# Expert weights in 2 MiB transfers of 16 KB rows, with six ring places instead of twelve

## The chip, the cores and the metric

The kernel runs on one core of one Trainium2 chip. The metric is the device time of one execution in microseconds, as the median of several runs. One further execution was taken by the hardware profiler; the rows below are its.

## What is computed

Two layers of a diffusion backbone over 256 latent tokens and 256 context tokens with 1024 channels. Each layer mixes tokens (Fourier, neighbourhood attention, short convolution) and then channels. The channel mixer of layer 0 is a dense SwiGLU, that of layer 1 is a router with eight experts, of which each latent token uses two:

```python
def moe(h, w_router, w_gate, w_up, w_down):
    logits = (h @ w_router).astype(jnp.float32)
    top_val, top_idx = lax.top_k(logits, TOP_K)
    ...
    out = jnp.zeros_like(h)
    for e in range(N_EXPERTS):
        out = out + gates[..., e:e + 1] * swiglu(h, w_gate[e], w_up[e], w_down[e])
    return out
```

One expert has a gate and an up matrix of 1024 x 3584 and a down matrix of 3584 x 1024, all float32: 42 MiB. All eight experts are read in every execution, 336 MiB. The change is in how these weights reach SBUF; what is computed from them stays.

## The kernel before

**Steps.** An expert's 3584 inner channels are worked in seven chunks of 512 (FE = 7), so there are 56 steps (expert, chunk). A step uses three blocks of weights of 2 MiB: gate, up and, one step later, down. Experts are of two kinds, ABABABAB. An A expert may hold 128 tokens; its weights are split into a high and a low part (`split`, line 181: ACT copies to `wh`, DVE subtracts to `wl`), and each product is three matmuls (`mm3`, line 188). A B expert holds 64 tokens; PE reads its float32 weights from the raw tile directly (lines 1263 and 1303). `expert_steps` (line 266) gives the order: four A steps first, then B and A steps in turn, then the last four B steps.

**A step** (`step`, line 1342, in the function `experts`) does `gate_up` for its own chunk and then `down` for the step before it. Inside `gate_up`, PE also transposes the previous step's product (`turn`, line 1271; PE transposes, L1275). That product is the DVE multiplication at line 1269. After the last A chunk of an expert with a successor pair, `gather` (line 1197, matmuls at L1210) picks the rows of the next two experts. PE, ACT and DVE run in the order in which the program is written (`manual_schedule`).

**Weights.** `expert_plan` (line 274) lists the loads in the order in which PE uses them: every block as two halves of 1 MiB, 128 rows of 8 KB. Half n goes to place n mod 15. The places are twelve tiles of their own (`ring`, RING = 12, line 951) and the three buffers of `net.wraw`, which served the earlier layers. The first twelve loads are issued by POOL (the `aside` argument), all others by SP, in the order of the plan (`Stream.load`, line 73). Up to fifteen halves are asked for ahead of the one being made ready; the DMA into a place waits until the half before it there has been read. For an A half that is when DVE has finished the second of its two splits, for a B half when PE has done its matmuls. SP's queue is in order, so a load that waits for its place holds up those behind it.

**Splitting ahead.** `Stream.make` (line 98) writes the splits of A weights into ACT's and DVE's order up to four units (quarter blocks of 1024 columns) ahead of PE, because there are four `wh`/`wl` pairs. So the first splits of an A block `down` stand in the order of ACT and DVE before the multiplication of that A step, while PE uses that block only after the next B step's gate and up products.

**An expert's result.** `scatter` (line 1311) writes an expert's output to a tile with the tag `y` in the pool `pre`. The same memory held the router's input before (`Route.start`, line 1033).

The functions that the change touches, and those that call them, follow.

Of the kernel before, what the change touches and what calls it, by code (L numbers as in the profile page):

```python
# [8 lines left out]
F32 = mybir.dt.float32  # L9
# [10 lines left out]
P = 128  # L20
# [9 lines left out]
NE = 8  # L30
FE = 7
# [5 lines left out]
CAPS = (128, 128, 128, 64, 64, 64, 64)  # L37

LEAD = 4
RING = 12  # L40
SCRATCH = 2048
HALVES = 5

# [16 lines left out]
class Stream:  # L60


    def __init__(self, net, plan, ahead, parts, aside=0, before=8):

        self.aside, self.before = aside, before
        self.net, self.plan, self.ahead, self.parts = net, plan, ahead, parts
        self.units = [(i, j) for i, (_, _, nu, _, _) in enumerate(plan) for j in range(nu)]
        self.loaded, self.raws, self.halves = 0, {}, 0
        self.at, self.made, self.count, self.ready = 0, 0, 0, {}
        self.alive, self.kept, self.used = [], {}, []  # L70
        self.hold = len(self.units)

    def load(self, upto):
        nc = self.net.nc
        while self.loaded < min(upto, len(self.plan)):
            _, src, _, n, pool = self.plan[self.loaded]
            if pool is None:
                if self.halves == HALVES:
                    return
                self.halves += 1  # L80
            eng = nc.gpsimd if self.loaded < self.aside else nc.sync
            src = src() if callable(src) else src
            if pool is None:
                t = self.net.halves()
                for j in range(2):
                    eng.dma_start(t[j], src[:, j * D:(j + 1) * D])
            else:
                t = pool.tile([P, 2048], F32, tag="raw", name="raw")
                eng.dma_start(t[:, :n], src)
            self.raws[self.loaded] = t  # L90
            self.loaded += 1
# [6 lines left out]
    def make(self):  # L98

        net = self.net  # L100
        while self.made < self.hold:
            i, j = self.units[self.made]
            _, _, nu, n, _ = self.plan[i]
            whole = nu == 1
            if not whole and len(self.alive) == len(self.parts) or self.made > self.at + self.before:
                return
            self.load(i + self.ahead)
            if i not in self.raws:
                return
            raw = self.raws[i]  # L110
            if whole:
                self.ready[self.made] = raw
            else:
                m = n // nu
                wh, wl = self.parts[self.count % len(self.parts)]
                h = wh.tile([P, 1024], F32R, tag="wh", name="wh")
                lo = wl.tile([P, 1024], F32R, tag="wl", name="wl")
                net.split(h[:, :m], lo[:, :m], raw[:, j * m:(j + 1) * m])
                self.ready[self.made] = (h, lo)
                self.alive.append(self.made)  # L120
                self.count += 1
            if j == nu - 1:
                del self.raws[i]
            self.made += 1
# [141 lines left out]
def expert_steps(kinds):  # L266

    a, b = ([(e, f) for e in range(NE) if kinds[e] == x for f in range(FE)] for x in "AB")
    if not b:
        return a  # L270
    return a[:LEAD] + [x for y in zip(b, a[LEAD:]) for x in y] + b[len(a) - LEAD:]


def expert_plan(a, pools, kinds, expert):

    plan, n = [], 0
    steps = expert_steps(kinds)
    for i in range(len(steps) + 1):
        srcs = []
        if i < len(steps):  # L280
            srcs += [(x, *steps[i], hf) for x in "gu" for hf in range(2)]
        if i > 0:
            srcs += [("d", *steps[i - 1], hf) for hf in range(2)]
        for x, e, f, hf in srcs:
            src = lambda x=x, e=e, f=f, hf=hf: a[f"moe_{x}"][expert(e), f, hf]
            plan.append(((x, e, f), src, 2 if kinds[e] == "A" else 1, 2048, pools[n % len(pools)]))
            n += 1
    return plan


def build(nc, tc, a, out):
    with ExitStack() as es:
        net = Net(nc, tc, es, a)
# [651 lines left out]
        with late(name="own", bufs=8, side="right") as own:  # L945
            with late(name="den1", bufs=1) as den, late(name="act1", bufs=3) as act, late(name="tog", bufs=8) as tog:
                x = mixing(act, den, tog, tog, own, 1, 6, route.shifts)
            first.close()
            more = lambda **kw: es.enter_context(late(**kw))

            ring = [more(name=f"ring{i}", bufs=1) for i in range(RING)]
            pre = more(name="pre", bufs=1)
            pools = ring + [net.wraw] * 3
            parts = [(net.wh, net.wl)] * 4
            stream = lambda aside, kinds, expert: Stream(net, expert_plan(a, pools, kinds, expert), len(pools), parts,
                                                         aside, 20)
            route.start(pre, scales(1, 1, g2, 1))
            mixed(1, x, route.chunk)

# [99 lines left out]
def experts(net, pre, mo, res, mods, route, rt, ident, ones, tri, iot, sel8):  # L1059
# [176 lines left out]
    def run(st, kinds, more, Sums):  # L1236
# [7 lines left out]
        def gate_up(e, f, between):  # L1244
            pg = [net.bank(), net.bank()]
            t = sg[e, f] = net.t2()
            whole = kinds[e] == "B"
            n = 256 if whole else 512
            for i, name in enumerate("gu"):
                for kk in range(4):  # L1250
                    if not whole:
                        h, lo = st.next(name, e, f)
                        for j in range(2):
                            k, c = 2 * kk + j, slice(j * 512, j * 512 + 512)
                            net.mm3(pg[i], xa[0][:, k], xa[1][:, k], h[:, c], lo[:, c], k == 0, k == KD - 1)
                    else:

                        if kk % 2 == 0:
                            w = st.next(name, e, f)
                        for k in (2 * kk, 2 * kk + 1):  # L1260
                            for j in range(2):
                                c = (k % 4) * 512 + j * 256
                                nc.tensor.matmul(pg[i][j * half:(j + 1) * half, :256], xb[e][:, k], w[:, c:c + 256],  # L1263
                                                 start=k == 0, stop=k == KD - 1)
                    if (i, kk) in between:
                        between[i, kk]()
                if i == 0:
                    net.act(t[:, :n], pg[0][:, :n], AF.Silu)
            nc.vector.tensor_mul(t[:, :n], t[:, :n], pg[1][:, :n])  # L1269
# [14 lines left out]
        def down(e, f, between={}):  # L1284
            x = parts.pop((e, f))
            if f == 0:
                py[e] = [net.bank(), net.bank()]
            for n in range(2):
                for i in range(2):
                    if kinds[e] == "A":  # L1290
                        h, lo = st.next("d", e, f)
                        for j in range(2):
                            k, c = 2 * i + j, slice(j * 512, j * 512 + 512)
                            kc = slice(k * P, k * P + P)
                            net.mm3(py[e][n], x[0][:, kc], x[1][:, kc], h[:, c], lo[:, c],
                                    f == 0 and k == 0, f == FE - 1 and k == 3)
                    else:
                        if i == 0:
                            w = st.next("d", e, f)

                        for j in range(2):
                            k, c = 2 * j + i, i * P + j * half
                            nc.tensor.matmul(py[e][n][j * half:(j + 1) * half], x[:, c:c + half],  # L1303
                                             w[:, k * 512:(k + 1) * 512],
                                             start=f == 0 and i == 0, stop=f == FE - 1 and i == 1)
                    if (n, i) in between:
                        between[n, i]()
                if f == FE - 1:
                    scatter(e, n)
# [31 lines left out]
        y = {}  # L1341
# [52 lines left out]
def layout(i):  # L1394
# [4 lines left out]
    a = {}  # L1399
# [39 lines left out]
    a["router"][:, :, :NE] = i["moe_router"][0].reshape(KD, P, NE).transpose(1, 0, 2)  # L1439
    for n, s in (("moe_g", "moe_w_gate"), ("moe_u", "moe_w_up")):  # L1440
        w = i[s][0].reshape(NE, 2, 4, P, FE, 512)
        a[n] = c(w.transpose(0, 4, 1, 3, 2, 5).reshape(NE, FE, 2, P, 2048))
    w = i["moe_w_down"][0].reshape(NE, FE, 4, P, 2, 512)
    a["moe_d"] = c(w.transpose(0, 1, 4, 3, 2, 5).reshape(NE, FE, 2, P, 2048))


    rows = S // GW
# [44 lines left out]
```

## Time and profile before

| | us |
|---|---|
| median of three runs | 1854.37 |
| the three runs | 1853.98, 1854.37, 1857.76 |
| the profiled execution | 1857.7 |
| its span, first to last instruction | 1855.9 |
| PE busy in the span | 1827.5 (98%) |
| DVE busy | 1183.7 (64%) |
| ACT busy | 824.5 (44%) |
| mean granted TensorE clock | 0.996 |

DMA moved 514.69 MB, 277 GB/s on average. The span is what the rows of the profile are measured in: their times count from its first instruction. A busy PE is not a PE at its peak, since the ends of matmuls are modelled. An idle engine costs time only where the chain of waits runs through it.

### The profile page before, as it was taken

The numbers are of one execution on the slowest core, as the hardware profiler recorded it, in microseconds if no ns is written. First come the engines' busy times: TensorE is split into PE (matmuls) and PEld (weight loads), VectorE is DVE, ScalarE is ACT, GpSimd is POOL, SyncE is SP. The second block draws the span as 40 slices with busy tenths as digits, with TensorE's granted clock in tenths as the row PEclk, the third lists the DMA queues.
The fourth block names the chain that finished last, engine by engine and source line by source line (L and its number), as shares of the span: only waits on it lengthen the run. The fifth ranks groups of instructions, "written<-read, shape, count | busy, mean of one in ns | idle before, by whom it ended". The sixth has DMA issues, their size and how long they took to land.

```text
span 1855.9 us, 26261 instructions
## 1 busy us (share of the span) xinstructions
PE 1827.5 (98%) x10254; PEld 1438.4 (78%) x10254; DVE 1183.7 (64%) x1725; ACT 824.5 (44%) x1179; POOL 23.4 (1%) x49
## 2 busy tenths in 40 slices
PE   7999999999999999999999999999999999999997
PEld 5787888888888888898999877677676767667664
DVE  5658677759767474668567866565665656566542
ACT  3546322334222223355446755454554545455431
POOL 0000000000000000001000000000000000000000
PEclk9999999999999999999999999999999999999998
DMA  9322344434547463344756899999999999999994
GB/s 368 114 91 91 133 162 159 177 141 159 204 145 261 161 238 114 123 148 144 279 184 267 339 383 421 416 421 421 420 420 421 421 421 421 421 421 421 421 421 201
DMA packets 74355, 514.69 MB, mean 277 GB/s; under 512 B 8432, under 2 KB 8560, under 8 KB 14448
## 3 DMA queue, kind: packets, MB, share of 16 engines
q1 hardware_dynamic: 69840, 491.84, 67.4%
q0 software_dynamic: 4240, 20.97, 3.2%
q8 instruction: 82, 1.34, 0.3%
q14 instruction: 49, 0.40, 0.1%
q10 hardware_dynamic: 144, 0.13, 0.0%
HBM read 509.76 MB, written 1.05 MB: 275 GB/s over the span
## 4 chain that ended last, share of the span: by engine, by line
PE 92%; DMA 5%; DVE 2%; ACT 1%; issue 0%; SPq 0%; ACTq 0%; DVEq 0%
PE ps L190 23%; PE ps L191 23%; PE ps L192 23%; PE ps L1263 10%; PE ps L1303 5%; DMA raw<-in_moe_d 2%; PE ps L1275 1%; DMA raw<-in_moe_u 1%; DMA raw<-in_moe_g 1%; PE ps L641 1%; PE ps L617 1%; PE ps L653 1%; PE ps L1210 1%; DMA res<-in_xT 1%; PE ps L1332 0%; PE ps L342 0%
## 5 line engine op out<-in xcount | busy, mean ns | idle before, releaser
L183 ACT CAST wh<-raw 128x1024 fp32r<-128x1024 f32 (+1 forms) x524 | 544.9, 1049 | 654.3 <-PE ps L191 367.2
L186 DVE TENSOR_TENSOR wl<-raw,wh 128x1024 fp32r<-128x1024 f32 (+1 forms) x524 | 630.9, 1218 | 240.1 <-ACT wh L183 206.8
L190 PE MATMUL ps<-hh,wh 128*128 128x512 f32 (+1 forms) x1024 | 361.3, 355 | 1.4 <-ACT hh L170 1.4
L191 PE MATMUL ps<-hl,wh 128*128 128x512 f32 (+1 forms) x1024 | 361.0, 353 | 0.9 <-DVE hl L433 0.6
L192 PE MATMUL ps<-hh,wl 128*128 128x512 f32 (+1 forms) x1024 | 360.6, 353 | 0.0
L190 PEld LDWEIGHTS ps<-hh,wh 128*128 128x128 f32 x1024 | 192.7, 189 | 30.1 <-issue 2.0
L191 PEld LDWEIGHTS ps<-hl,wh 128*128 128x128 f32 x1024 | 193.6, 189 | 27.5 <-DVE hl L433 1.5
L192 PEld LDWEIGHTS ps<-hh,wl 128*128 128x128 f32 x1024 | 193.5, 189 | 26.6
L1263 PE MATMUL ps<-raw,xb 128*64 128x256 f32 x1792 | 208.8, 384 | 0.0
L1263 PEld LDWEIGHTS ps<-raw,xb 128*64 128x64 f32 x1792 | 125.8, 138 | 77.1 <-issue 20.8
L363 DVE CUSTOM_DVE_ANT_0 junk<-raw,csb,early 128x1024 bf16<-128x1024 f32 x128 | 164.2, 1282 | 32.7 <-DMA raw<-in_w_at 30.3
L190 PE MATMUL ps<-wh,xh 128*128 128x512 f32 x448 | 177.3, 396 | 0.0
L192 PE MATMUL ps<-wh,xl 128*128 128x512 f32 x448 | 174.7, 390 | 0.0
L191 PE MATMUL ps<-wl,xh 128*128 128x512 f32 x448 | 174.7, 390 | 0.0
L1269 DVE TENSOR_TENSOR t<-t,ps 128x512 f32<-128x512 f32 (+1 forms) x56 | 30.8, 551 | 113.0 <-PE ps L1263 113.0
L1303 PE MATMUL ps<-raw,t 128*64 128x512 f32 x448 | 102.2, 598 | 0.0
L192 PEld LDWEIGHTS ps<-wh,xl 128*128 128x128 f32 x448 | 84.1, 188 | 17.7
L191 PEld LDWEIGHTS ps<-wl,xh 128*128 128x128 f32 x448 | 84.2, 188 | 16.3
L190 PEld LDWEIGHTS ps<-wh,xh 128*128 128x128 f32 x448 | 84.2, 188 | 16.3
L190 PE MATMUL ps<-wh,t 128*128 128x512 f32 x224 | 90.3, 403 | 0.0
L192 PE MATMUL ps<-wh,t 128*128 128x512 f32 x224 | 87.4, 390 | 0.0
L191 PE MATMUL ps<-wl,t 128*128 128x512 f32 x224 | 87.3, 390 | 0.0
(233 smaller groups left out, 2156.4 us busy)
## 6 DMA issues: line engine op xcount, KB each, us to landing
raw<-in_moe_d SPq DMA_DIRECT2D x110, 1024.0 KB, 16.2
raw<-in_moe_u SPq DMA_DIRECT2D x108, 1024.0 KB, 16.2
raw<-in_moe_g SPq DMA_DIRECT2D x106, 1024.0 KB, 15.6
raw<-in_w_at SPq DMA_DIRECT2D x40, 1024.0 KB, 4.9
raw<-in_w_gb SPq DMA_DIRECT2D x32, 1024.0 KB, 4.9
raw<-in_w_gu SPq DMA_DIRECT2D x22, 1024.0 KB, 4.9
raw<-in_w_in SPq DMA_DIRECT2D x20, 1024.0 KB, 5.0
a<-in_w_a SPq DMA_DIRECT2D x16, 512.0 KB, 11.4
```

Of the source, the lines that this page charges most:

```text
L183: c = self.nc.scalar.copy(h, src)
L186: self.nc.vector.tensor_sub(lo, src, h.bitcast(F32))
L190: nc.tensor.matmul(ps, wh, xh, start=start, stop=False)
L191: nc.tensor.matmul(ps, wh, xl, start=False, stop=False)
L192: nc.tensor.matmul(ps, wl, xh, start=False, stop=stop)
L363: nc.vector.tensor_tensor_reduce(junk, w[:, j * D:(j + 1) * D], csb[s], 1.0, bada[:, l, m + j:m + j + 1], ALU.mult, ALU.add, mods[l][:, m ...
L617: nc.tensor.matmul(banks[qt][:, :nk], qs[2 * c + j][:, i, s * S + qt * P:s * S + qt * P + P], ks[2 * c + j][:, k0:T], start=i == 0, stop=i ...
L641: nc.tensor.transpose(tr[:, i * P:(i + 1) * P], p[:, i * P:(i + 1) * P], ident)
L653: nc.tensor.matmul(po[64 * j:64 * j + 64, :S], v(k0 + i)[:, (2 * c + j) * 64:(2 * c + j) * 64 + 64], pts[c, s, j][:, i, :], start=i == 0, ...
L1263: nc.tensor.matmul(pg[i][j * half:(j + 1) * half, :256], xb[e][:, k], w[:, c:c + 256], start=k == 0, stop=k == KD - 1)
L1269: nc.vector.tensor_mul(t[:, :n], t[:, :n], pg[1][:, :n])
L1303: nc.tensor.matmul(py[e][n][j * half:(j + 1) * half], x[:, c:c + half], w[:, k * 512:(k + 1) * 512], start=f == 0 and i == 0, stop=f == FE ...
```

## The change

Gate, up and down blocks go as whole transfers of 2 MiB, 128 rows of 16 KB, to six ring places (RING = 6, each twice as wide). Of every five blocks one still goes as two halves of 8 KB rows to the three buffers of `net.wraw`. Early on, one block more goes so; its second half goes to the place of an expert's result, in `pre`. A list `turns` says for each load which load had its place before it; the load is asked for as soon as that one has been made ready. The arrays in HBM are laid out to match, and the matmuls of B experts find their columns in a tile of either width. With RING = 6, POOL issues the first six loads, SP all others.

```diff
-RING = 12
+RING = 6
...
-                t = pool.tile([P, 2048], F32, tag="raw", name="raw")
+                tag = "y" if pool.name == "pre" else "raw"
+                t = pool.tile([P, max(n, 2048)], F32, tag=tag, name="raw")
                 eng.dma_start(t[:, :n], src)
...
-            self.load(i + self.ahead)
+            upto = i + self.ahead
+            if self.turns:
+                upto = self.loaded
+                while upto < len(self.plan) and self.turns[upto] < i:
+                    upto += 1
+            self.load(upto)
...
-def expert_plan(a, pools, kinds, expert):
-
-    plan, n = [], 0
+def expert_plan(a, ring, single, once, kinds, expert):
+    plan, before, where = [], [], {}
     steps = expert_steps(kinds)
+    n = rings = singles = 0
     for i in range(len(steps) + 1):
-        srcs = []
+        blocks = []
         if i < len(steps):
-            srcs += [(x, *steps[i], hf) for x in "gu" for hf in range(2)]
+            blocks += [(x, *steps[i]) for x in "gu"]
         if i > 0:
-            srcs += [("d", *steps[i - 1], hf) for hf in range(2)]
-        for x, e, f, hf in srcs:
-            src = lambda x=x, e=e, f=f, hf=hf: a[f"moe_{x}"][expert(e), f, hf]
-            plan.append(((x, e, f), src, 2 if kinds[e] == "A" else 1, 2048, pools[n % len(pools)]))
+            blocks += [("d", *steps[i - 1])]
+        for x, e, f in blocks:
+            split = kinds[e] == "A"
+            if n < len(ring) or (n - len(ring)) % 5 > (n == len(ring) + 1):
+                src = lambda x=x, e=e, f=f: a[f"moe_{x}"][expert(e), f]
+                places = [(src, 4, 4096, ring[rings % len(ring)], ("ring", rings % len(ring)))]
+                rings += 1
+            else:
+                places = []
+                for j in range(2):
+                    src = lambda x=x, e=e, f=f, j=j: a[f"moe_{x}"][expert(e), f, :, j * 2048:j * 2048 + 2048]
+                    if n == len(ring) + 1 and j:
+                        places.append((src, 2, 2048, once, "once"))
+                    else:
+                        places.append((src, 2, 2048, single, ("single", singles % 3)))
+                        singles += 1
+            for src, units, width, pool, place in places:
+                before.append(where.get(place, -1))
+                where[place] = len(plan)
+                plan.append(((x, e, f), src, units if split else 1, width, pool))
             n += 1
-    return plan
+    return plan, before
...
-                        if kk % 2 == 0:
+                        if kk == 0 or kk == 2 and w.shape[-1] == 2048:
                             w = st.next(name, e, f)
...
-                                c = (k % 4) * 512 + j * 256
+                                c = k * 512 % w.shape[-1] + j * 256
...
-                        if i == 0:
+                        if i == 0 and (n == 0 or w.shape[-1] == 2048):
                             w = st.next("d", e, f)
...
-                                             w[:, k * 512:(k + 1) * 512],
+                                             w[:, o:o + 512],
...
-        a[n] = c(w.transpose(0, 4, 1, 3, 2, 5).reshape(NE, FE, 2, P, 2048))
+        a[n] = c(w.transpose(0, 4, 3, 1, 2, 5).reshape(NE, FE, P, 4096))
...
-    a["moe_d"] = c(w.transpose(0, 1, 4, 3, 2, 5).reshape(NE, FE, 2, P, 2048))
+    a["moe_d"] = c(w.transpose(0, 1, 3, 4, 2, 5).reshape(NE, FE, P, 4096))
```

## Rows read from the trace of the kernel before

**Rows 1.** The page: busy tenths and DMA rate in 40 slices of the span.

```profile
PE   7999999999999999999999999999999999999997
...
GB/s 368 114 91 91 133 162 159 177 141 159 204 145 261 161 238 114 123 148 144 279 184 267 339 383 421 416 421 421 420 420 421 421 421 421 421 421 421 421 421 201
```

**Rows 2.** The chain that ended last: start us, us, what.

```profile
1308.32 3.58 PE ps L1303 x16
...
1514.19 3.58 PE ps L1303 x16
...
1550.04 19.47 DMA raw<-in_moe_d
...
1721.48 1.89 PE ps L1303 x8
...
1762.26 20.80 DMA raw<-in_moe_d
1783.17 1.05 ACT wh L183
1784.24 1.23 DVE wl L186
1785.47 0.61 DVE t L1269
```

**Rows 3.** PE's timeline, late waits: start us, us, ..., idle before and releaser.

```profile
1574.93 0.47 PE L1210 MATMUL ps<-of,rh 128*128 128x192 f32 x2 [1.16 <-DVE t L1269]
...
1755.27 0.66 PE L1275 MATMUL ps<-early,t 128*128 128x128 f32 x4 [0.45 <-DVE t L1269]
...
1786.12 0.66 PE L1275 MATMUL ps<-early,t 128*128 128x128 f32 x4 [1.89 <-DVE t L1269]
```

**Rows 4.** Windows: stretch, length, PE, PEld, DVE, ACT, POOL busy, PEclk, DMA share, GB/s.

```profile
1020.00:1100.00 80.00, 80.00 (x413) 64.98 (x413) 64.77 (x77) 56.67 (x67) 0.00 (x0) 1.00 0.90 351
...
1786.90:1790.20 3.30, 3.30 (x18) 1.91 (x17) 0.99 (x2) 0.50 (x1) 0.00 (x0) 0.50 1.00 417
```

**Rows 5.** DMA in 12 to 18 us (4 KB rows), then in 1300 to 1500.

```profile
GB/s 137 437 328 410 437 437 437 410 355 437 437 437 410 355 410 382 437 410 437 410 437 410 437 410 382 437 355 410 328 410 410 410 437 437 437 437 355 437 437 410
DMA packets 665, 2.43 MB, mean 404 GB/s; under 512 B 80, under 2 KB 80, under 8 KB 658
...
DMA packets 11538, 84.13 MB, mean 421 GB/s; under 512 B 1278, under 2 KB 1278, under 8 KB 1278
```

**Rows 6.** SP's timeline, issues of expert weights, late: start us, us.

```profile
1739.91 2.82 SPq L89 DMA_DIRECT2D raw<-in_moe_u  x2
1744.88 0.33 SPq L89 DMA_DIRECT2D raw<-in_moe_d  x1
```

**Rows 7.** DVE's timeline, low parts of the split, early in the expert phase.

```profile
1037.15 8.04 DVE L186 TENSOR_TENSOR wl<-raw,wh 128x1024 fp32r<-128x1024 f32 x7
...
1047.49 2.36 DVE L186 TENSOR_TENSOR wl<-raw,wh 128x1024 fp32r<-128x1024 f32 x2 [0.57 <-ACT wh L183]
```

**Rows 8.** SP's timeline in 1034.9:1035.1, and that issue's time to landing.

```profile
1034.96 0.36 SPq L89 DMA_DIRECT2D raw<-in_moe_g  x1
...
raw<-in_moe_g SPq DMA_DIRECT2D x1, 1024.0 KB, 4.8
```

**Rows 9.** PE's timeline, first gate half of the first B expert.

```profile
1077.79 1.95 PE L1263 MATMUL ps<-raw,xb 128*64 128x256 f32 x16
```

**Rows 10.** Two issues on SP's timeline, and each one's time to landing.

```profile
1135.84 0.33 SPq L89 DMA_DIRECT2D raw<-in_moe_u  x1
...
raw<-in_moe_u SPq DMA_DIRECT2D x1, 1024.0 KB, 10.5
...
1344.75 0.33 SPq L89 DMA_DIRECT2D raw<-in_moe_d  x1
...
raw<-in_moe_d SPq DMA_DIRECT2D x1, 1024.0 KB, 16.7
```

**Rows 11.** PE's timeline, last bank of the gather for experts 4 and 5.

```profile
1367.74 0.39 PE L1210 MATMUL ps<-of,rh 128*128 128x192 f32 x2
```

More of the change, by code (lines that the diff above doesn't have):

```diff
@@ L60, with __init__ @@
 class Stream:
-    def __init__(self, net, plan, ahead, parts, aside=0, before=8):
-        self.aside, self.before = aside, before
+    def __init__(self, net, plan, ahead, parts, aside=0, before=8, turns=None):
+        self.aside, self.before, self.turns = aside, before, turns
         self.net, self.plan, self.ahead, self.parts = net, plan, ahead, parts
@@ L952, in build, with stream @@
             pre = more(name="pre", bufs=1)
-            pools = ring + [net.wraw] * 3
             parts = [(net.wh, net.wl)] * 4
-            stream = lambda aside, kinds, expert: Stream(net, expert_plan(a, pools, kinds, expert), len(pools), parts,
-                                                         aside, 20)
+            def stream(aside, kinds, expert):
+                plan, turns = expert_plan(a, ring, net.wraw, pre, kinds, expert)
+                return Stream(net, plan, 0, parts, aside, 20, turns)
             route.start(pre, scales(1, 1, g2, 1))
@@ L1302, in down @@
                             k, c = 2 * j + i, i * P + j * half
+                            o = (4 * n + k) * 512 % w.shape[-1]
                             nc.tensor.matmul(py[e][n][j * half:(j + 1) * half], x[:, c:c + half],
-                                             w[:, k * 512:(k + 1) * 512],
+                                             w[:, o:o + 512],
                                              start=f == 0 and i == 0, stop=f == FE - 1 and i == 1)
```

## The prediction, made before the changed kernel was run

> **What bounds the kernel now.** I read the page's slices first, to see where DMA and TensorE are full together. In [rows 1] PE shows 9 tenths in all but two slices, and from the 25th slice, about 1,113 us, the DMA engines move 416 to 421 GB/s without a dip. That is the expert phase, the only one the change touches after the start of its loads. A full PE and a full DMA cannot both be the bound, so the chain of waits comes next. It gives the start of the same matmul group, the down product of a B expert, one expert pair apart [rows 2]: 1308.32, 1514.19 and 1721.48. The first period is 205.87 us, the second 207.29, so 1.42 us appeared in the second. A period that repeats and holds no DMA piece is PE's own pace; a DMA piece enters the chain first at 1550.04. So PE sets the time, and DMA, a little slower, eats its lead until weights come late.
>
> The reader is to see in [rows 3] how late. The wait that costs is that of the halves of `down` weights of an A expert. They are split by ACT and DVE while PE still does the preceding gate-ups, well ahead of their use. When the last of them lands late, DVE's multiplication (L1269) stands behind the split, and PE waits for it: at the gather (L1210) by 1.16 us at 1574.93, and at the transposes (L1275) by 0.45 and 1.89 us, 2.3 together. The chain names the landing behind the last: issue 1762.26, 20.80 us, then one ACT split, one DVE split, the multiplication, PE [rows 2]. After that wait the granted clock is 0.50, the 1.2 GHz level, from 1786.9 to 1790.2 [rows 4]; half of some 3.4 us is 1.7 us lost. In all, 1.42 + 2.3 + 1.7 = **5.4 us** of the span are late weights. The rest of the expert phase is PE work which the change leaves alone, so 5.4 us is all that it can win, 0.3% of the time.
>
> **The change, part by part.**
>
> *Longer rows.* Both kernels move 336 MiB. By the new plan 134 blocks go as 2 MiB and 34 as two halves: 202 transfers instead of 336, later four blocks of five with 16 KB rows. No row shows a 16 KB row of weights. The nearest are 4 KB and 8 KB rows with all engines full: 404 GB/s in the window 12 to 18 us (578 packets under 8 KB besides 80 tiny ones) and 421 GB/s in 1300 to 1500 [rows 5]. Over 16 engines that is 4096 B x 16 / 404 GB/s = 162 ns a packet, and 311 ns for 8192 B. If a packet costs a fixed part and a part by its bytes, the fixed part is 2 x 162 - 311 = 13 ns, and a 16 KB row takes 2 x 311 - 13 = 609 ns. With eight rows to an engine in 2 MiB, a MiB takes 8 x 609 / 2 = 2.44 us instead of 2.485 (SP's issues stand 4.97 us apart for two, [rows 6]). I take 2.44. The dear end is no gain, 2.485. The cheap end is the best slice of the 4 KB window, 437 GB/s, so 2.40. With one block of five in halves, the mean is 0.8 x 2.44 + 0.2 x 2.485 = 2.449, so 0.036 us saved per MiB.
>
> *Places.* Fifteen places of 1 MiB become six of 2 MiB and three of 1 MiB, plus one early half in the expert result's place. The bytes are nearly the same, but the order of reuse is not. Before, each load waits for the half 15 before it. Now the second half of each fifth block waits for the half 11 before it, and SP's queue stands in order behind it. The first time this bites is the first gate block of the first B expert: it takes two single places whose halves (up, step 2) DVE finishes splitting near 1045.1 (the seven splits from 1037.15) and 1048.7 [rows 7]. Before, that load left at 1034.96 [rows 8]. From 1045.2, with 2.4 us from issue to the first byte (4.8 alone, [rows 8], less 2.485), DMA starts at 1047.6. The next 11 MiB (eight in long rows) take 8 x 2.44 + 3 x 2.485 = 27.0, to 1074.6. Then the second half of a `down` block waits for the first half of that gate block, which PE reads until 1079.7 [rows 9]; data flow again at 1082.1. The 29 MiB after that (24 in long rows) take 71.0, to 1153.1. In the kernel before, the same last half, issued at 1135.84, lands 10.5 later, at 1146.3 [rows 10]. So the new plan **loses 6.8 us of lead** here, while PE has weights in hand. DMA was only 0.90 busy in 1020 to 1100 before [rows 4]: it, too, waited for places, but less.
>
> *Regaining it.* From there DMA is full in both, and 0.036 us per MiB comes back: after 86 MiB (the gather near 1367) the lag is 6.8 - 3.1 = 3.7 us, after 170 MiB (1574) it is 0.7, after 254 MiB (1785) DMA is 2.3 us ahead.
>
> *One landing instead of two.* A block counts as landed only when both halves are there. Where the second half's landing was the late one, one ACT split (1.05) and one DVE split (1.23) stood between it and the multiplication. Now three DVE splits do: 1.05 + 3 x 1.23 + 0.61 = 5.4 us from landing to PE, by the single durations in [rows 2].
>
> *The sum* at the three places where it comes close. Near 1367: the half issued at 1344.75 lands 16.7 later, at 1361.5 [rows 10]; plus 3.7 and 5.4 is 1370.6. PE wants it for the last eight matmuls of the gather, which began at 1367.74 without a wait [rows 11]. That is 2.9 us of wait, and since 1.89 us were enough to bring the clock down, 1.7 more: 4.6. Near 1574: the second half lands at 1569.5 (issue 1550.04 and 19.47, [rows 2]) + 2.5 = 1572.0; plus 0.7 and 5.4 is 1578.1, wanted at 1574.93 - 1.16 = 1573.8. That is 4.3, inside the 4.6 already lost. Near 1785: 1783.1 - 2.3 + 5.4 = 1786.2, wanted at 1786.12 less the 3.8 us of earlier waits, 1782.3: 3.9, again inside. So 4.6 us are lost instead of 5.4: **0.8 us faster**, nothing that can be told.
>
> *Small parts together.* The half in the result's place waits until the router's input is read, which is over before the expert's first matmuls; its split comes after 1049.85 [rows 7], and that distance covers it. On POOL six issues take the place of twelve, into the same memory in pairs, and the same distance covers them. The matmuls, splits and their order stay: only offsets into wider tiles change. The chain before holds no landing after 1783 [rows 2], so the last transfers were not waited for; a whole block lands when its second half did, now 2 us sooner, so I cost its single landing at nothing there, 2.5 us (one MiB) if that cover is gone.
>
> The profiled execution took 1857.7 us, 1.8 more than its span; less 0.8 that is 1856.9. The median of the runs, 1854.4, lies 3.3 lower, so I forecast **1853.6**.
>
> **Rivals.** *Faster: the lead does not matter or comes back sooner.* At 437 GB/s the mean is 2.417 us, 0.068 saved per MiB. The same working gives a lag of 5.8 us near 1150, 0.0 near 1367 (1361.5 + 5.4 = 1366.9, in time) and DMA ahead later. All 5.4 us go: 1849.0. For it: the single slices at 437 [rows 5]. Against it: no long window holds that rate. It decides from about 0.05 us saved per MiB. The Trainium skill (DMA: Bandwidth & Descriptors, "Where 436 GB/s comes from") sets the ceiling of the ports at 435 GB/s; as an estimate from it, a MiB takes at least 2.41 us, and this rival is then just within reach.
>
> *Slower: long rows move no faster.* The place is DMA's queue after 1150. The lag is then 1154.2 - 1146.3 = 7.9 us and stays. Near 1785 PE waits 1783.1 + 7.9 + 5.4 - 1782.3 = 14.1 us in all instead of 5.4 (clock losses before it lie inside; one behind it adds 1.7): 1863 to 1865. For it: [rows 5] show no rate above 421 over a long window. It decides where less than about 0.02 us per MiB is saved: there the sum is 4 us over now. The Trainium skill (same page, "Specifications") gives about 358 GB/s as what HBM yields one core, by which no row length would help; the trace disagrees, with 421.
>
> *The change doesn't do what it says:* if 16 KB rows are cut into 8 KB packets, it is the case above. The packet count would tell: 134 blocks x 128 = some 17,000 fewer where the rows go whole.
>
> **How the numbers follow.** A measurement here can tell about 0.2%, 3.7 us, from no change. Forecast and its neighbours, 1850.7 to 1858.1: 0.45. The faster rival: 0.25. The slower one, with its half-way cases (from 1858.1): 0.30. The forecast's own range, for a lag off by 2 us either way, is 1851 to 1857. The range of 8 in 10 goes to the faster rival's end, 1849, and to the slower one's near end, 1863.
>
> **What would show it.** Right: about 428 GB/s in long windows; an idle DMA near 1035 to 1047 and 1075 to 1082; PE waits at a gather near 1367 and few at 1785. Wrong: 421 GB/s still, or no idle DMA near 1040; a wait that grows to over 10 us near 1785; or PE waiting for B weights themselves, which this working leaves out.

## The result, and the profile after

The changed kernel takes 1871.2 us (median of six runs, 1864.7 to 1872.1) beside 1856.3 us for the kernel before on the same chip: a ratio of 1.0078, interval 1.0067 to 1.0088. It is **14.5 us slower**. The prediction said 1853.6, and its range ended at 1863. The profiled execution took 1872.1 us, its span is 1870.4 (before: 1855.9).

The page of the changed kernel, the lines that answer to [rows 1], and its packets:

```profile
PE   7999999999999999999999999999999999999997
...
GB/s 365 112 92 91 133 160 161 180 132 165 196 160 251 151 261 110 99 143 160 262 199 289 299 348 427 419 424 427 425 381 411 425 426 427 393 422 423 427 425 206
DMA packets 55055, 514.65 MB, mean 275 GB/s; under 512 B 6288, under 2 KB 6416, under 8 KB 12304
```

The rows do go whole: 19,300 packets fewer than before (74,355). And DMA is faster where it is full, 419 to 427 GB/s a slice, mostly 424 and more, against 420 and 421. But now there are dips, 381 and 411 between 1356 and 1450, 393 between 1590 and 1637, where [rows 1] showed 416 at the least.

The chain of the changed kernel, with the lines that answer to [rows 2] (L1303 of before is now L1332, L183 L189, L186 L192, L1269 L1297, L1275 L1303, L1210 L1238, L1263 L1291):

```profile
1105.32 3.58 PE ps L1332 x16
...
1312.30 3.58 PE ps L1332 x16
...
1320.11 21.53 DMA raw<-in_moe_d
1341.74 1.05 ACT wh L189
1342.82 3.50 DVE wl L192 x3
1346.32 0.61 DVE t L1297
...
1353.13 17.96 DMA raw<-in_moe_d
...
1526.67 3.58 PE ps L1332 x16
...
1566.98 17.21 DMA raw<-in_moe_d
...
1738.78 3.58 PE ps L1332 x16
...
1774.62 21.71 DMA raw<-in_moe_d
```

The periods of the down group are now 206.98, 214.37 and 212.11 us, where PE's own pace was 205.87. Seven transfers of `down` blocks stand in the chain, the first issued at 1150.77. Behind a landing there are now one ACT split, three DVE splits and the multiplication, as the prediction had it.

PE's timeline of the changed kernel, the waits that answer to [rows 3]:

```profile
1165.77 0.36 PE L1238 MATMUL ps<-of,rh 128*128 128x192 f32 x1 [0.87 <-DVE t L1297]
...
1346.97 0.33 PE L1303 MATMUL ps<-early,t 128*128 128x128 f32 x1 [1.33 <-DVE t L1297]
...
1376.42 0.47 PE L1238 MATMUL ps<-of,rh 128*128 128x192 f32 x2 [3.15 <-DVE t L1297]
...
1501.25 0.33 PE L1303 MATMUL ps<-early,t 128*128 128x128 f32 x1 [2.02 <-DVE t L1297]
...
1589.52 0.53 PE L1238 MATMUL ps<-of,rh 128*128 128x192 f32 x1 [3.12 <-DVE t L1297]
...
1801.66 0.33 PE L1303 MATMUL ps<-early,t 128*128 128x128 f32 x1 [0.65 <-DVE t L1297]
```

Windows of the changed kernel (columns as in [rows 4]):

```profile
1020.00:1040.00 20.00, 20.00 (x94) 16.60 (x93) 19.07 (x32) 16.00 (x17) 0.00 (x0) 1.00 0.57 211
...
1060.00:1080.00 20.00, 20.00 (x92) 16.55 (x91) 17.59 (x16) 16.27 (x18) 0.00 (x0) 1.00 0.58 229
...
1100.00:1150.00 50.00, 50.00 (x292) 34.12 (x291) 27.72 (x32) 22.67 (x27) 0.00 (x0) 1.00 1.01 425
1376.80:1380.20 3.40, 3.40 (x13) 1.88 (x14) 1.74 (x8) 2.07 (x6) 0.00 (x0) 0.50 0.92 381
1380.00:1387.00 7.00, 7.00 (x53) 3.54 (x51) 1.91 (x2) 0.74 (x3) 0.00 (x0) 0.99 0.37 111
1588.40:1595.20 6.80, 5.68 (x18) 3.02 (x20) 4.46 (x11) 3.58 (x13) 0.00 (x0) 0.50 1.02 435
```

Late weights now cost 0.87 + 1.33 + 3.15 + 2.02 + 3.12 + 0.65 = 11.1 us of waiting, and half of the 3.4 and 5.7 us in which PE worked at a granted clock of 0.50 (the first 1.1 us of the last window lie still in the wait): 15.7 in all, against the 5.4 of before. That is 10.3 of the 14.5 us by which the spans differ. Another 2.9 lie ahead of the first B `down` group (1105.25 on PE's timeline, 1102.39 before), where the kernels hardly differ; in the profiles of the runs below this start moves between 1099.5 and 1105.3 with no relation to the edits that can be seen. So the experiments are read from that group to the end of the span: 753.5 us before, 765.1 after, 11.6 more.

The window of 1380 to 1387 is the one that the prediction did not have in it: DMA at 0.37, 111 GB/s, right behind the wait of 3.15 us. SP's timeline has the issue that was being waited for, and PE's the matmuls that hold its place:

```profile
1066.82 16.14 SPq L90 DMA_DIRECT2D raw<-in_moe_d  x2
...
1362.47 22.39 SPq L90 DMA_DIRECT2D raw<-in_moe_d  x2
```

```profile
1383.67 0.81 PE L1291 MATMUL ps<-raw,xb 128*64 128x256 f32 x6
```

Block 76, a `down` block, is one of the fifth blocks. Its second half sat at the head of SP's queue until 1384.9. Its place, 11 halves back, is read by gate matmuls of a B expert, which come after the gather. PE waited at the gather for a late landing, so it freed this place late, and everything behind it in SP's queue left late: the DMA engines ran dry.

### The profile page after: what moved, and what is told of

The parts are those of the page before. It is cut to its first block, busy times and chain, and to the rows that moved or that the text cites. A ratio compares the mean times of both kernels' runs of the same rounds, so it can differ in the third digit from the quotient of the medians.

```text
span 1870.4 us, 25625 instructions
## 1 busy us (share of the span) xinstructions
PE 1833.7 (98%) x10254; PEld 1442.5 (77%) x10254; DVE 1181.5 (63%) x1725; ACT 821.3 (44%) x1179; POOL 20.2 (1%) x43
## 4 chain that ended last, share of the span: by engine, by line
PE 88%; DMA 8%; DVE 3%; ACT 1%; issue 0%; SPq 0%; ACTq 0%; DVEq 0%
PE ps L196 22%; PE ps L197 22%; PE ps L198 22%; PE ps L1291 10%; DMA raw<-in_moe_d 7%; PE ps L1332 5%; DVE wl L192 1%; PE ps L1303 1%; PE ps L667 1%; PE ps L643 1%; PE ps L679 1%; PE ps L1238 1%; DMA res<-in_xT 1%; ACT wh L189 1%; PE ps L1361 0%; PE ps L368 0%
## 5 line engine op out<-in xcount | busy, mean ns | idle before, releaser
L189 ACT CAST wh<-raw 128x1024 fp32r<-128x1024 f32 (+1 forms) x524 | 541.7, 1047 | 683.5 <-PE ps L197 367.6
L192 DVE TENSOR_TENSOR wl<-raw,wh 128x1024 fp32r<-128x1024 f32 (+1 forms) x524 | 630.6, 1218 | 280.4 <-ACT wh L189 251.2
L1291 PE MATMUL ps<-raw,xb 128*64 128x256 f32 x1792 | 207.1, 381 | 0.0
L1291 PEld LDWEIGHTS ps<-raw,xb 128*64 128x64 f32 x1792 | 124.9, 137 | 76.3 <-issue 20.3
L1332 PE MATMUL ps<-raw,t 128*64 128x512 f32 x448 | 105.0, 612 | 0.0
L1297 DVE TENSOR_TENSOR t<-t,ps 128x512 f32<-128x512 f32 (+1 forms) x56 | 30.8, 549 | 110.9 <-PE ps L1291 110.9
```

What stands on the lines that cost most here:

```text
L189: c = self.nc.scalar.copy(h, src)
L192: self.nc.vector.tensor_sub(lo, src, h.bitcast(F32))
```

## The experiments

The lag is the landing of one half beside the same half of the kernel before, both from the start of the first B `down` group. Halves 61, 147, 231 and 315, counted from 0, are those of the prediction near 1146, 1361, 1570 and 1783.

| kernel | ratio, 95% interval | group to end, us | lag at half 61, 147, 231, 315 |
|---|---|---|---|
| before | 1 | 753.5 | 0, 0, 0, 0 |
| after | 1.0078 [1.0067, 1.0088] | 765.1 | 8.6, 6.8, 9.5, 10.4 |
| e1 every seventh | 1.0004 [0.9993, 1.0016] | 753.2 | 3.9, 1.6, 0.1, -3.5 |
| e2 two landings | 1.0073 [1.0049, 1.0098] | 763.9 | 9.3, 9.3, 11.8, 12.0 |
| e3 eleven places | 1.0133 [1.0110, 1.0156] | 778.5 | 10.5, 14.3, 19.9, 24.6 |
| e4 A's down in halves | 1.0041 [1.0027, 1.0056] | 760.9 | 8.6, 6.8, 7.8, 6.3 |
| e5 = e1 and e4 | 1.0004 [0.9994, 1.0014] | 750.6 | 4.6, 3.6, 1.2, -2.1 |
| e6 sevenths early | 1.0061 [1.0040, 1.0082] | 766.5 | 4.0, 7.5, 11.6, 11.2 |
| e7 sevenths late | 1.0004 [0.9995, 1.0013] | 752.3 | 8.5, 5.8, 2.9, -0.7 |
| e8 = e1 and e2 | 1.0022 [1.0013, 1.0031] | 757.2 | 4.6, 4.5, 5.0, 4.5 |
| e9 sevenths late, whole | 1.0027 [1.0016, 1.0038] | 757.0 | 8.4, 5.8, 5.3, 2.2 |
| e10 lead kept | 0.9987 [0.9979, 0.9996] | 751.4 | 3.6, 1.9, -0.2, -3.2 |

**e1: every seventh block in halves.** By the plan, the place of a second half then comes round after 15 halves, not 11, and no load waits for a half closer than 13 before it (a ring block with one block in halves since its place was last filled).

```diff
-            if n < len(ring) or (n - len(ring)) % 5 > (n == len(ring) + 1):
+            if n < len(ring) or (n - len(ring)) % 7 > (n == len(ring) + 1):
```

> The changed kernel, but every seventh block instead of every fifth goes as two halves to the single places; then no half waits for one closer than 13 halves before it (changed kernel: 11), while even more blocks go as 2 MiB with one landing. Theory A (the short reuse distance of the single places loses lead near 1080 us and lets DMA run dry after each wait of PE): no idle DMA near 1385 us, late-weight waits fall from some 16 us to under 6, time 1850 to 1858. Theory B (a block that lands only as a whole comes too late for the splits, whatever the places): waits stay, 1866 or more. Theory C (long rows bring too little): 1866 or more as well, as the rate is the same.

The whole loss is gone (1.0004). The lag starts at 3.9 and is made up by half 231. Windows of this run, and its worst wait:

```profile
1300.00:1500.00 200.00, 199.49 (x1153) 140.50 (x1152) 119.59 (x138) 100.30 (x127) 0.00 (x0) 1.00 1.01 426
1500.00:1700.00 200.00, 197.22 (x1127) 139.38 (x1127) 121.49 (x135) 103.28 (x130) 0.00 (x0) 1.00 1.00 424
...
1574.00:1580.00 6.00, 5.39 (x32) 2.75 (x34) 3.95 (x10) 3.07 (x10) 0.00 (x0) 1.00 0.91 381
```

```profile
1574.61 0.36 PE L1238 MATMUL ps<-of,rh 128*128 128x192 f32 x1 [2.78 <-DVE t L1297]
```

So the distance of reuse decides; the nine blocks that go whole besides are worth some 0.8 us by the prediction's prices (18 MiB at 2.485 less 2.44). That says nothing yet on which part of its effect costs: the lead lost at 1035 to 1082, or something later.

**e2: 2 MiB places, but two transfers of 8 KB rows into each,** so that the order of places stays as in the change, while rows and landings are those of before.

```diff
-                eng.dma_start(t[:, :n], src)
+                for c in range(0, n, min(n, 2048)):
+                    eng.dma_start(t[:, c:c + min(n, 2048)], src[:, c:c + min(n, 2048)])
```

> The changed kernel with its places and their order, but each 2 MiB block comes as two transfers of 8 KB rows into the two halves of its tile, so that rows and landings are those of the kernel before. Theory A: the idle DMA near 1068 to 1082 us stays and the 0.02 to 0.03 us per MiB of the long rows are gone too, so 1866 to 1872. Theory B: back to the time before, 1853 to 1859. Theory C: the same as B, or a little above the changed kernel.

1.0073, which can't be told from the change. With the short distance, what the long rows bring and what the single landing costs come to nothing together, as far as these runs can tell.

**e3: the kernel before with eleven places,** nothing else of the change in it.

```diff
-RING = 12
+RING = 8
```

> The kernel before, halves of 1 MiB with 8 KB rows, with 8 ring places instead of 12, so that every load waits for the half 11 before it instead of 15. Theory A: the reuse distance alone makes it slow, 1862 to 1872. Theories B and C: rows and landings are those of before, within 3 us of 1856.

Slower by 24 us, more than the change, since here every load waits for the half 11 before it. The waits view of this run (us in total, times, longest) against 1.2 and 2.3 us before:

```profile
PE ps L1210 <- DVE t L1269: 10.6, 3, 4.3
PE ps L1275 <- DVE t L1269: 9.5, 8, 1.6
```

So neither long rows nor single landings are needed for such a loss. And the lag grows from 10.5 to 24.6 with rows of the old length: lead that is lost does not merely stay lost. But eleven places also hold 4 MiB less than fifteen, so this run doesn't part the distance from the bytes in flight; the change and e1, with the same bytes, do.

**e4: the `down` blocks of A experts in two transfers** (two landings), all else as changed.

```diff
-                eng.dma_start(t[:, :n], src)
+                m = 2048 if self.plan[self.loaded][0][0] == "d" and self.plan[self.loaded][2] == 4 else n
+                for c in range(0, n, m):
+                    eng.dma_start(t[:, c:c + m], src[:, c:c + m])
```

> The changed kernel, but the down blocks of A experts come to their ring places as two transfers of 1 MiB, so that their first half can be split while the second is on its way; all else as in the changed kernel. Theory A: 2 to 4 us less at each late landing, but the lost lead stays, so 1861 to 1868. Theory B: most of the loss goes, 1853 to 1859.

About half of the loss goes. **e5** has this edit and that of e1:

> Every seventh block to the single places, and the down blocks of A experts in two transfers of 1 MiB; a version that might beat both kernels. Theory A: the places no longer cost lead, and the 2.8 us wait that was left at the third gather with every seventh block was that of a whole landing (three splits after it), so it goes: 1850 to 1855. If the single landing is not what is left, no change from every seventh alone, 1855 to 1858.

Beside e1 it changes nothing that can be told; its worst wait is 1.83 us where e1 has 2.78. So with most of the lead kept the landing costs little or nothing.

**e6 and e7: the distance changed in time.** e6 has every seventh block in halves up to block 33 and every fifth from there; e7 the reverse.

```diff
-            if n < len(ring) or (n - len(ring)) % 5 > (n == len(ring) + 1):
+            if n < len(ring) or (n - len(ring)) % (7 if n < 34 else 5) > (n == len(ring) + 1):
...
+            if n < len(ring) or (n - len(ring)) % 5 * (n < 34) + (n - 3) % 7 * (n >= 34) > (n == len(ring) + 1):
```

> The changed kernel, but the first three blocks after the start that go to single places are spaced by seven; from block 36 on every fifth as in the changed kernel. Theory A1 (what costs is the lead lost near 1080 us): nearly all is regained, 1854 to 1859. Theory A2 (what costs is the short distance later, which lets DMA run dry after every wait of PE): 1862 or more.

> The reverse: every fifth block up to block 31, so that the lead is lost as in the changed kernel, then every seventh. Theory A1: the lag of some 8 us is there at the first two gathers, 1860 to 1867. Theory A2: no idle DMA after the waits and the lag regained, 1854 to 1859.

e6 is inconclusive: where the spacing changes, two ring blocks wait for places only six blocks back, and DMA is idle for some 4 us near 1167, so the lead is lost there instead (lag 4.0, then 7.5). But it shows the hole behind the gather once more, with the lag going from 7.5 at half 147 to 12.4 at half 153:

```profile
1378.00:1392.00 14.00, 14.00 (x88) 6.96 (x87) 2.71 (x5) 2.94 (x7) 0.00 (x0) 0.82 0.58 219
```

e7 is clear: the early lead is lost exactly as in the changed kernel (8.5 at half 61), then 9.1 us come back over 254 MiB, 0.036 us per MiB, and the ratio is 1.0004. But it has a second difference. With seven as the period (an expert pair has 42 blocks), the `down` block that each gather waits for (31, 73, 115, 157) is in halves, every time.

**e8: every seventh block in halves, and two transfers into each 2 MiB place** (the edits of e1 and e2).

> Every seventh block to the single places, but all ring blocks in two transfers of 8 KB rows: rows and landings as in the kernel before, places as in the every-seventh kernel. It weighs the long rows (0.03 us saved per MiB, some 8 us over the phase) against their single landing (2.4 us at a late block). If the long rows are worth what their rate says, this is slower than every seventh alone, 1858 to 1864; if the single landing costs as much as they bring, the same, 1855 to 1858; if more, 1850 to 1854.

The lag stays at 4.5 to 5.0: with 8 KB rows nothing is regained. Against e1 the long rows, less what their single landing costs, are worth 1.0022 less 1.0004, some 3 us; the two intervals just overlap.

**e9: as e7, but with the gathers' blocks whole** (sevenths at 36, 43, 50, ...).

```diff
-            if n < len(ring) or (n - len(ring)) % 5 > (n == len(ring) + 1):
+            if n < len(ring) or (n - len(ring)) % 5 * (n < 34) + (n - 1) % 7 * (n >= 34) > (n == len(ring) + 1):
```

> The changed kernel with every fifth block in halves up to block 31 and every seventh from block 36 on (36, 43, 50, ...). So the lead is lost early as in the changed kernel (the lag behind the kernel before near 1150 is 8 to 9 us), the distance of reuse is 13 halves from then on, and, unlike in the run with the late sevenths, the down block that each later gather waits for (steps 73, 115 and 157 of the plan) comes whole, in one landing. Theory D (the short distance is the cost, because every late place lets the DMA engines run dry again): no hole in DMA after 1150, the lag falls by 0.03 us per MiB, ratio 0.999 to 1.002, about 1855 to 1860, one wait of under 2 us near 1367. Theory L (the lost lead together with the single landing at the gathers is enough, and the run with the late sevenths was saved by its halves there): a wait of 2.5 to 4 us near 1371 with the clock at 0.5 behind it, ratio 1.003 to 1.006, about 1862 to 1868.

Between the two theories: 1.0027. The wait of theory L is there, and so is the full DMA of theory D behind it. DVE's and PE's timelines and windows of e9:

```profile
1365.83 3.50 DVE L192 TENSOR_TENSOR wl<-raw,wh 128x1024 fp32r<-128x1024 f32 x3 [4.23 <-ACT wh L189]
1369.24 0.68 DVE L1297 TENSOR_TENSOR t<-t,ps 128x512 f32<-128x512 f32 x1
```

```profile
1369.98 0.53 PE L1238 MATMUL ps<-of,rh 128*128 128x192 f32 x1 [3.11 <-DVE t L1297]
```

```profile
1369.00:1375.80 6.80, 5.82 (x18) 2.94 (x20) 4.31 (x11) 3.45 (x12) 0.00 (x0) 0.53 1.00 423
...
1380.00:1400.00 20.00, 20.00 (x121) 15.81 (x118) 13.35 (x19) 11.12 (x15) 0.00 (x0) 1.00 1.01 428
```

The same place in e7, whose block comes in halves: ACT's split of the third quarter starts when the second half lands, and only one DVE split and the multiplication are left.

```profile
1367.03 1.05 ACT L189 CAST wh<-raw 128x1024 fp32r<-128x1024 f32 x1 [0.48 <-DMA raw<-in_moe_d]
```

```profile
1369.99 0.47 PE L1238 MATMUL ps<-of,rh 128*128 128x192 f32 x2 [0.87 <-DVE t L1297]
```

The chains of e9 and of e7 have the transfer that was waited for:

```profile
1347.41 17.23 DMA raw<-in_moe_d
```

```profile
1347.12 19.81 DMA raw<-in_moe_d
```

The block of e9 landed at 1364.64 and the multiplication began 4.6 us later; in e7 the second half landed at 1366.93 and the multiplication began at 1369.26, 2.3 later. From the first B `down` group (1099.78 in e9, 1102.03 in e7) both landings are 264.9 us away, so only the work behind the landing differs. Its 2.3 us are the difference of the waits, 3.11 less 0.87, and the clock fell in e9 alone. The changed kernel waits as long at this gather as e9, 3.15 us, and its clock falls for less time. What it has besides is the distance of 11 behind the wait, the hole of 1380 to 1387, and three more waits, 5.8 us in sum, where e9 has one of 1.23. Across the hole, from half 147 to 153, its lag grows from 6.8 to 10.4; in e9 it goes from 5.8 to 5.6.

**e10: a version with the lead kept.** Halves at blocks 6, 7, 13, 18, 24 and from 31 on every seventh.

```diff
-            if n < len(ring) or (n - len(ring)) % 5 > (n == len(ring) + 1):
+            if n not in (6, 7, 13, 18, 24) and (n < 31 or n % 7 != 3):
```

> The changed kernel with halves at blocks 6, 7, 13, 18, 24 and from 31 on at every seventh (31, 38, 45, ...): distance 13 nearly from the start, so the lead is kept but for one place of 11 at block 18, and the down blocks that the gathers wait for (31, 73, 115, 157) come in halves. If the late weights of the kernel before (5.4 us of its span) are all that can be won, and the lead, the distance and the landing are what decides them: waits of under 2 us in sum, no clock at 0.5 in the expert phase, ratio 0.997 to 0.9995, about 1851 to 1855. If the waits that stay come from the order of the splits on DVE and not from late landings: the same as every seventh from the start, ratio 0.9995 to 1.0015.

0.9987, 2.4 us faster than the kernel before: the only version whose interval lies below 1. Its windows and the two waits of the expert phase that are left:

```profile
1300.00:1500.00 200.00, 200.00 (x1157) 141.05 (x1157) 120.95 (x138) 100.60 (x129) 0.00 (x0) 1.00 1.01 426
1500.00:1700.00 200.00, 199.09 (x1132) 141.20 (x1132) 122.18 (x135) 104.24 (x131) 0.00 (x0) 1.00 1.01 426
```

```profile
1575.67 0.36 PE L1238 MATMUL ps<-of,rh 128*128 128x192 f32 x1 [0.91 <-DVE t L1297]
...
1755.99 0.33 PE L1303 MATMUL ps<-early,t 128*128 128x128 f32 x1 [0.45 <-DVE t L1297]
```

## Why the prediction was wrong

**The bound: right.** PE sets the pace, and late `down` weights of A experts are what costs. Waits and clock account for 10.3 of the 11.6 us from the first group on; the other 1.3 were not traced.

**Longer rows: right.** 2.449 us per MiB were forecast, 428 GB/s; e1's window shows 426, 2.46. Where DMA stays full, e7 regains the 0.036 us per MiB, and e8 shows that it is the rows. The Trainium skill (DMA: Bandwidth & Descriptors, "Specifications") gives about 358 GB/s as one core's limit at HBM, half of what two cores share. The traces here, of one core that runs alone, disagree: windows of 100 us with DMA full show up to 427. The ceiling of 435 in "Where 436 GB/s comes from" agrees, as no window of 100 us or more went over 427.

**Places: right in kind, too small.** The two idle stretches are there (DMA 0.57 and 0.58), and the second place comes free where predicted: 1079.7 and the start's 2.9 make 1082.6, SP's row ends at 1083.0. Between the stretches DMA was not full, as the working had it, but 0.78 busy (1049.9 to 1077.9; 0.89 at the same place before). The lead lost is 8.6 us, not 6.8. Where the other 1.8 come from was not settled. (A slip besides: 4.8 less 2.485 is 2.3 us to the first byte, not 2.4.)

**One landing: right.** Forecast 5.4 us from landing to PE instead of some 3; e9 and e7 show 2.3 us between the two at the same matmuls.

**Regaining it: this step failed.** It said "From there DMA is full in both, and 0.036 us per MiB comes back". That holds for e7, but in the changed kernel the short distance comes round with every fifth block. A wait of PE frees such a place late, SP's in-order queue holds all loads behind it, DMA runs dry and lands later still. Between halves 147 and 153 the lag rose from 6.8 to 10.4 us, across the hole of 1380 to 1387; at half 315 it was 10.4 where -2.3 was forecast. The prediction followed the distance once, at its first bite, and then treated the lead as a number that only the rate changes. The rivals made the same assumption; the slower one had the right sign with the wrong mechanism, since the rows were faster.

**The sum: two further errors.** It worked out three places, and of these only the first came out: 2.9 us of wait and 1.7 for the clock, where the changed kernel has 3.15 and 1.7; e9, which has the early loss and the single landings without the later short distances, waits 3.11 us there and loses some 2.7 to the clock. Even this place is partly luck: the lag there was 6.8 us, not 3.7, and PE came to these matmuls 2.7 us later than before (1373.27 less 1105.25 against 1367.74 less 1102.39), 2.2 of them in waits at 1165 and 1346 that the sum does not have. The two errors nearly cancel. It took later waits to lie inside the earlier ones; with the loss fed back they add up. And it left out the transposes of each earlier period (1346.97 and 1501.25, 3.35 us together), where a single landing with three splits behind it is late too.

Put together from the ratios: the short distance after block 36 costs 14.5 - 5.0 = 9.5 us (after against e9), the single landings at the gathers 4.3 (e9 against e7), and the rest, the early lead, 3.2 (e7 against e10; their intervals touch, so this part is weak): 17 us in all from e10 to the change. They are not independent: the landing is worth 4.3 here, 6.9 with the short distance (after against e4), and nothing that can be told with most of the lead kept (e1 against e5).

## What to carry to other kernels

When places of different sizes share one in-order queue of loads, work out the shortest distance of reuse over the whole plan, not the sum of the bytes: it sets how far the engine that frees places may fall behind before the DMA engines run dry. Where it is short (here 11 halves instead of 15, while 13 at the least did no harm in e1), a wait of the bound engine frees a place late, the late load breeds the next wait, and what a faster transfer rate brings is lost again. A larger transfer also makes its first part land as late as its last: here 2.3 us more work behind the landing, which cost nothing that could be told with most of the lead kept, and about 4 us of the time where it was lost.

## What the runs showed of the hardware that was not expected

The length of PE's wait does not decide alone whether the granted clock falls. Before, it fell to 0.50, the 1.2 GHz level, after 1.89 us [rows 3, 4]. In e1 it stayed at 1.00 after 2.78 us (window 1574 to 1580 above), and in the changed kernel after 2.02, as this window shows:

```profile
1501.20:1508.00 6.80, 6.75 (x54) 4.68 (x56) 6.27 (x12) 0.97 (x2) 0.00 (x0) 1.00 1.00 426
```

It fell after 3.15, 3.12 and, in e9, 3.11, once for 3.4 and twice for about 6.8 us, of which about one lies still in the wait. So two waits of equal length, at the same gather, cost 1.7 and some 2.7 us more. The prediction's "1.89 us were enough" was no rule. What else decides was not tried.
